# Half-size products from the fifth block on in the two feed-forward layers, with another way to make the first output weights

## The chip, the cores and the metric

The program runs on one core of a Trainium2 chip. The metric is device time in microseconds (us) from launch to end; the figure for the kernel before is the median of three runs. The engines are named as the profile names them: PE multiplies matrices, PEld loads weights into it, DVE and ACT work element by element, POOL is the general engine that here issues the adding DMA, and SP issues the plain loads and stores. A line such as L485 is a line of the profiled kernel's file.

## What is computed

The reference is one layer of a decoder over 512 prompt tokens and 8 x 4 new tokens: a half-step SwiGLU feed-forward (FF1), a token mixer (RWKV-7 heads beside differential attention), a second half-step SwiGLU (FF2), each between two root-mean-square norms. The change lies in the two feed-forwards:

```python
def rms_norm(x, g, eps):
    xf = x.astype(jnp.float32)
    y = xf * lax.rsqrt(jnp.mean(xf * xf, axis=-1, keepdims=True) + eps)
    return (y * g.astype(jnp.float32)).astype(x.dtype)

def swiglu(x, w_in, w_out):
    gate, up = jnp.split(x @ w_in, 2, axis=-1)
    return (jax.nn.silu(gate) * up) @ w_out
```

`x` has 544 rows of 1024, `w_in` is 1024 x 5632, `w_out` 2816 x 1024, all float32.

## The kernel before, in words

**Tiles and exactness.** The tokens lie along the free dimension in two halves of 272, so each product is a matmul of a 128 x 128 piece of weight with 128 x 272 of input. A float32 product is made of three products in the round format fp32r: `whi` is the weight rounded (ACT copy), `wlo` the rest (raw minus `whi`), and the input is split in the same way into high and low (`split`, L164 to L166: ACT copy, DVE subtract). `dot` issues for each of the pieces high x high (L148) and high x low (L149) and, after all of these, low x high (L154). So a weight's low is asked for late in its product.

**A feed-forward** (`ff`, from L431) has 22 blocks of 128 hidden columns; a block needs a gate column block and an up column block. Blocks are gathered in `GROUPS`; after the blocks of a group, the group's hidden tiles `hd0`, `hd1` (one set for each token half, each split into high and low) are multiplied with the group's rows of `w_out` (`products`, L377) and added to the eight output tiles `y` of each half. In the first group the output is copied from PSUM by ACT (L615), in later ones it is added by DVE (L620).

**The two kinds of block.** The first group's blocks are multiplied plainly: 2 weights x 2 halves x 8 pieces x 3 = 96 matmuls a block. Blocks 0 and 1 go through `opening`, blocks 2 to 5 through the loop at L569 (two blocks a pass, `ws` holds their four weights, token half outside, block inside). All other blocks go through `seven` (L509), a form of Strassen's and Winograd's method: the block's gate and up columns against the upper and lower half of the 1024 rows make a 2 x 2 matrix of weights, and the input's halves by tokens and rows another; seven products of half the depth (`product`, 4 pieces x 3 = 12 matmuls each, 84 in all) and some additions give the same four results.

**What `seven` needs.** Of the weights, `load` brings `b` (called `wraw`), `t1` (two 256 KB loads of the same piece on SP's queue, then one adding DMA of 512 KB on POOL's queue, L473) and `b22`; `factors` makes the high and low of `b`, `b22`, `t1` and of `t2`, a sum that DVE makes (L497, L498). The low of `b` is made by an ACT copy with scale -1 onto which a DMA on POOL's queue adds the weight from memory (L494, L495); the other lows are DVE subtractions (L487). Of the input it needs seven sets: `scaled` (L412) multiplies the rows of `h` by norm and gain in place (L417) and splits three of four quarters into the tiles `fa`; `mixtures` (L425) makes four sums and differences (L430) and splits them into `sh`, `sl`. Both are generators that are stepped by other work: `scaled` by four steps behind each hidden tile of the passes of blocks 4 and 5 (L588 to L590), `mixtures` by two steps behind each output copy of the first group (L616).

**What sets the order.** The lines give a program order; a scheduler that simulates a timeline then sets each engine's order, from priorities, from due dependences and from `after(ins)`, which lets what follows be issued only after `ins`. Tiles of one name share a few buffers: four `whi`/`wlo`, three `wraw`, three `t1`, six hidden tiles in each half. A new weight's high and low wait until the one four places back has been read last.

**Names the change touches**: `GROUPS`, `split`, `weights` (whose argument `added` chooses the ACT copy and adding DMA at L121 and L122 over the DVE subtraction at L124), `products`, `mixtures`, `hidden`, `load`, `factors`, `seven`, the loop at L569 and `finish` (L613). `begin` and `midway` are what the two feed-forwards do beside their opening blocks: FF1 stores the input and prepares a table at `midway`.

Of the kernel before, what the change touches and what calls it, by code (L numbers as in the profile page):

```python
# [22 lines left out]
GROUPS = ((0, 6), (6, 11), (11, 16), (16, 22))  # L23
# [29 lines left out]
def build(ctx, tc, A):  # L53
# [109 lines left out]
    def split(pool, src, name, n=HALF, into=None, **kw):  # L163
        hi, lo = into or [pool.tile([128, n], FR, name=name + p, **kw) for p in "hl"]  # L164
        S.activation(hi, src, AF.Copy)
        V.tensor_tensor(lo, src, hi.bitcast(FT), op=OP.subtract)  # L166
# [14 lines left out]
    turn, last, latest, root = [0], [None], [None], [None]  # L181
# [195 lines left out]
    def products(wsrc, x, y, finish, per=1, wx=None, apart=False):  # L377
# [21 lines left out]
    def combined(pre, h, pool, xp):  # L399
# [25 lines left out]
        def mixtures():  # L425
            for k in range(KH):
                a11, a12, a21, a22 = h[0][:, k], h[0][:, KH + k], h[1][:, k], h[1][:, KH + k]
                for i, (dst, p, q, op) in enumerate(((a22, a22, a21, OP.subtract), (a21, a11, a21, OP.add),
                                                     (a11, a22, a11, OP.subtract), (a12, a12, a11, OP.add))):
# [8 lines left out]
    def ff(win, wout, pre, h, done, xp, end, lead=(), begin=None, midway=None, ahead_of_end=None):  # L438
        with ExitStack() as st:
# [7 lines left out]
            hid, made = [[], []], [None]  # L447
            wt = None

            def hidden(s, g, u, sign=1.0):  # L450
                S.activation(g, g, AF.Silu, scale=sign)
                made[0] = V.tensor_tensor(u, u, g, op=OP.mult).ins
# [10 lines left out]
            def load(j):  # L463
# [4 lines left out]
                for i in range(2):  # L468
                    nc.sync.dma_start(t1[:, i], win[j, 1, :, :512])
# [3 lines left out]
                G.dma_start(t1, bass.AP(tensor=src.tensor, offset=src.offset,  # L473
                                        ap=[[1024, 128], [128 * 1024 + 512, 2], [1, 512]]), accum_op=OP.add)
                loaded[j] = raw, t1, b22

            def factors(j):
# [16 lines left out]
                S.activation(lo, raw, AF.Copy, scale=-1.0)  # L494
                G.dma_start(lo, win[j, 0], accum_op=OP.add)  # L495
# [14 lines left out]
            def seven(j):  # L510
# [23 lines left out]
                r = half(abank)  # L534
                product(r, t1, 1, s3)
                g1 = add(gu_tile("ga"), r, u2)
                q = half(bank)
                product(q, t1, 0, s1)
# [13 lines left out]
            for gi, (j0, j1) in enumerate(GROUPS):  # L552
                if gi == 0:
# [17 lines left out]
                    behind = [None, None]  # L571
                    for j in range(2, j1, 2):
                        if midway and j == 4:
                            midway()
                        ws = [[weights(win[i, n], 1024, added=begin is None and i == 3) for n in range(2)] for i in (j, j + 1)]
# [1077 lines left out]
```

## Time and profile before

| | us |
|---|---|
| median of three runs | 1195.15 |
| the runs | 1193.9, 1195.15, 1203.37 |
| the profiled execution | 1195.1 |
| its span (first to last instruction) | 1193.3 |

The mean clock that PE was granted in the profiled execution was 0.989 of full speed. The span is what the profile resolves; 1.8 us lie outside it. In the page, the first line of an engine gives its busy time, the share of the span and its instructions; the groups give for each line what an engine did, how long one took, and how long the engine stood idle just before them and what ended the wait. In the view of windows each row has the start and end, the length, then busy time with number of instructions of PE, PEld, DVE, ACT and POOL, the clock that PE was granted, the share of the DMA engines in use and GB/s. In the timeline each row has start, length, engine, line, operation, tiles, count, and in brackets the idle time ahead and what ended it.

Two stretches matter: FF1's first group and its output (blocks from the start to 84.95 us, output from 84.95 to 122.50 us), and the same in FF2 (output from 875.27 to 912.82 us).

### The profile page before, as it was taken

The page shows a single profiled execution, that of the slowest core. Times are in us where ns is not written, and L with a number is a line of the kernel's source. Part 1 is how long each engine was busy: PE and PEld are TensorE (multiplying, and loading weights), DVE is VectorE, ACT ScalarE, POOL GpSimd, SP SyncE. Part 2 cuts the span into 40 slices and gives each one's busy share as a digit, 9 for nine tenths or more (in the row PEclk, how much of TensorE's full clock was granted, in tenths as well). Part 3 has the DMA queues.
Part 4 walks back from the last instruction along what each step waited for, and adds up shares of the span by engine and source line. Part 5 has one row for each costly group of instructions (what it writes and reads, how often), then busy time and mean ns, then how long its engine had stood idle before and what let it go on. Part 6 is the DMA issues. An engine that isn't in the chain of part 4 may idle for free. (4 is left out here: it accounts for less than half of the span.)

```text
span 1193.3 us, 25431 instructions
## 1 busy us (share of the span) xinstructions
PE 1166.6 (98%) x10020; PEld 1103.5 (92%) x10020; DVE 821.2 (69%) x1878; ACT 583.6 (49%) x1081; POOL 169.5 (14%) x228
## 2 busy tenths in 40 slices
PE   8999999999999999999999999999999999999995
PEld 8999999999999999989897645999999999999995
DVE  8794684775875777778525658788784766857856
ACT  6455552643645664443214546567455634525530
POOL 0001110110101165531000021100001201101001
PEclk9999999999999998899999999999999999999998
DMA  7328895884847456789426486554259876857532
GB/s 262 108 67 240 218 212 122 198 205 114 189 162 211 117 155 175 223 228 257 118 56 209 143 321 214 192 190 132 72 152 230 210 181 154 216 144 181 116 116 75
DMA packets 86089, 205.42 MB, mean 172 GB/s; under 512 B 9144, under 2 KB 20152, under 8 KB 84562
## 3 DMA queue, kind: packets, MB, share of 16 engines
q1 hardware_dynamic: 65954, 149.69, 37.7%
q0 software_dynamic: 17712, 49.65, 23.4%
q10 hardware_dynamic: 2304, 4.46, 1.0%
q8 instruction: 79, 1.29, 0.4%
q14 instruction: 40, 0.33, 0.1%
HBM read 186.12 MB, written 18.95 MB: 172 GB/s over the span
## 5 line engine op out<-in xcount | busy, mean ns | idle before, releaser
L118 ACT ACTIVATE whi<-wraw 128x1024 fp32r<-128x1024 f32 (+2 forms) x127 | 116.8, 923 | 164.3 <-PE mm L149 75.3
L148 PE MATMUL mm<-xh,whi 128*128 128x272 f32 x456 | 121.3, 296 | 3.1 <-ACT whi L645 2.0
L149 PE MATMUL mm<-xl,whi 128*128 128x272 f32 x456 | 120.6, 294 | 0.0
L124 DVE TENSOR_TENSOR wlo<-wraw,whi 128x1024 fp32r<-128x1024 f32 (+2 forms) x100 | 100.6, 1008 | 17.7 <-ACT whi L118 16.7
L148 PEld LDWEIGHTS mm<-xh,whi 128*128 128x128 f32 x456 | 87.7, 193 | 4.5 <-ACT whi L645 2.2
L473 POOL DMA_DIRECT2D t<-in_ff_in_dram x32 | 38.8, 1213 | 362.7 <-DMA t<-in_ff_in_dram 139.4
L149 PEld LDWEIGHTS mm<-xl,whi 128*128 128x128 f32 x456 | 87.8, 193 | 0.4 <-DVE xl L282 0.2
L519 DVE TENSOR_TENSOR ga<-pb,ga 128x272 f32<-128x272 f32 x140 | 61.1, 436 | 23.6 <-PE pb L508 21.2
L154 PE MATMUL mm<-xh,wlo 128*128 128x272 f32 x456 | 69.3, 291 | 0.2 <-DMA wlo<-in_w_in_dram 0.2
L620 DVE TENSOR_TENSOR y<-mm,y 128x272 f32<-128x272 f32 x66 | 29.0, 440 | 54.9 <-PE mm L154 54.5
L505 PE MATMUL pb<-sh,t1h 128*128 128x272 f32 x256 | 66.7, 288 | 0.0
L506 PE MATMUL pb<-sl,t1h 128*128 128x272 f32 x256 | 66.6, 287 | 0.0
L149 PE MATMUL mm<-hd1l,whi 128*128 128x272 f32 x242 | 62.7, 289 | 1.0 <-DVE hd1l L166 1.0
L154 PEld LDWEIGHTS mm<-xh,wlo 128*128 128x128 f32 x456 | 61.9, 190 | 0.9 <-DMA wlo<-in_w_in_dram 0.5
L485 ACT ACTIVATE t1h<-t 128x1024 fp32r<-128x1024 f32 x32 | 34.0, 1061 | 58.7 <-issue 32.5
L149 PE MATMUL mm<-hd0l,whi 128*128 128x272 f32 x242 | 62.6, 288 | 0.0
L148 PE MATMUL mm<-hd0h,whi 128*128 128x272 f32 x242 | 62.2, 288 | 0.0
L148 PE MATMUL mm<-hd1h,whi 128*128 128x272 f32 x242 | 62.1, 289 | 0.0
L148 PE MATMUL pb<-xh,whi 128*128 128x272 f32 x232 | 61.3, 294 | 0.0
L149 PE MATMUL pb<-xl,whi 128*128 128x272 f32 x232 | 60.5, 291 | 0.0
L505 PE MATMUL pb<-fa,whi 128*128 128x272 f32 x216 | 56.2, 288 | 0.0
L506 PE MATMUL pb<-fa,whi 128*128 128x272 f32 x216 | 56.2, 288 | 0.0
(510 smaller groups left out, 3625.1 us busy)
## 6 DMA issues: line engine op xcount, KB each, us to landing
wraw<-in_ff_in_dram SPq DMA_DIRECT2D x55, 512.0 KB, 4.7
wlo<-in_ff_in_dram POOLq DMA_DIRECT2D x34, 512.0 KB, 7.3
t<-in_ff_in_dram SPq DMA_DIRECT2D x64, 256.0 KB, 3.6
t<-in_ff_in_dram POOLq DMA_DIRECT2D x32, 512.0 KB, 6.0
wraw<-in_w_in_dram SPq DMA_DIRECT2D x26, 512.0 KB, 8.0
wlo<-in_w_in_dram POOLq DMA_DIRECT2D x25, 512.0 KB, 8.3
wraw<-in_ff_out_dram SPq DMA_DIRECT2D x32, 384.0 KB, 3.1
wraw<-in_ff_out_dram SPq DMA_DIRECT2D x32, 320.0 KB, 3.2
```

The source lines that it names most:

```text
L118: S.activation(hi, raw, AF.Copy)
L124: V.tensor_tensor(lo, raw, hi.bitcast(FT), op=OP.subtract)
L148: T.matmul(ps, hi, xs[k][0], start=k == 0, stop=False)
L149: latest[0] = T.matmul(ps, hi, xs[k][1], start=False, stop=False).ins
L154: latest[0] = T.matmul(ps, wcols(w, k0 + k)[1], xs[k][0], start=False, stop=k == n - 1).ins
L473: G.dma_start(t1, bass.AP(tensor=src.tensor, offset=src.offset, ap=[[1024, 128], [128 * 1024 + 512, 2], [1, 512]]), accum_op=OP.add)
L485: S.activation(hi, src, AF.Copy)
L505: T.matmul(ps, c, x[k][0], start=k == 0, stop=False)
L506: T.matmul(ps, c, x[k][1], start=False, stop=False)
L519: V.tensor_tensor(dst, p, q, op=op)
L620: V.tensor_tensor(y[s][m], ps, y[s][m], op=OP.add)
```

## The change

**Groups.** The first group has four blocks rather than six, the others six. Blocks 4 and 5 go from 96 to 84 matmuls, and the loop at L569 is gone but for its first pass; the output weights of the first group are 128 x 512 rather than 128 x 768 (256 KB rather than 384 KB).

**Input.** `scaled` is stepped behind the hidden tiles of blocks 2 and 3, each step after the low of the hidden tile before (`made[0]`, now set in `split`). `mixtures` goes set by set rather than piece by piece; its steps come after the last low made.

**First output weights.** Their lows are made with `added`: an ACT copy with scale -1 and an adding DMA of 256 KB on POOL's queue, eight in each feed-forward, in place of a DVE subtraction.

**First seven-product block.** Its `t1` is summed by two DVE additions of 128 x 512 rather than by the adding DMA (and one of two loads falls away), and the low of its `b` is a DVE subtraction.

**Order in `seven`.** The products `r` and `q` (of `t1`) come ahead of the first of `t2`.

```diff
-GROUPS = ((0, 6), (6, 11), (11, 16), (16, 22))
+GROUPS = ((0, 4), (4, 10), (10, 16), (16, 22))
...
-        V.tensor_tensor(lo, src, hi.bitcast(FT), op=OP.subtract)
+        made[0] = V.tensor_tensor(lo, src, hi.bitcast(FT), op=OP.subtract).ins
...
-            ws.append(weights(wsrc(u), per * n * 128, wx and wx[u // 2]))
+            ws.append(weights(wsrc(u), per * n * 128, wx and wx[u // 2], added))
...
-            for k in range(KH):
-                a11, a12, a21, a22 = h[0][:, k], h[0][:, KH + k], h[1][:, k], h[1][:, KH + k]
-                for i, (dst, p, q, op) in enumerate(((a22, a22, a21, OP.subtract), (a21, a11, a21, OP.add),
+            for i in range(4):
+                for k in range(KH):
+                    a11, a12, a21, a22 = h[0][:, k], h[0][:, KH + k], h[1][:, k], h[1][:, KH + k]
...
-                for i in range(2):
+                first = j == GROUPS[0][1]
+                for i in range(1 if first else 2):
                     nc.sync.dma_start(t1[:, i], win[j, 1, :, :512])
...
+                if first:
+                    V.tensor_tensor(t1[:, 1], t1[:, 0], b22, op=OP.add)
+                    V.tensor_tensor(t1[:, 0], t1[:, 0], raw[:, :512], op=OP.add)
+                else:
+                    G.dma_start(t1, bass.AP(tensor=src.tensor, offset=src.offset,
+                                            ap=[[1024, 128], [128 * 1024 + 512, 2], [1, 512]]), accum_op=OP.add)
...
-                S.activation(lo, raw, AF.Copy, scale=-1.0)
-                G.dma_start(lo, win[j, 0], accum_op=OP.add)
+                if j == GROUPS[0][1]:
+                    V.tensor_tensor(lo, raw, hi.bitcast(FT), op=OP.subtract)
+                else:
+                    S.activation(lo, raw, AF.Copy, scale=-1.0)
+                    G.dma_start(lo, win[j, 0], accum_op=OP.add)
...
+                r = half(abank)
+                product(r, t1, 1, s3)
+                q = half(bank)
+                product(q, t1, 0, s1)
                 p = half(acc_tile)
                 product(p, t2, 0, s2)
...
-                    for j in range(2, j1, 2):
-                        if midway and j == 4:
-                            midway()
+                    if midway:
+                        midway()
...
+                            with after(behind[0] if behind else None):
+                                for _ in range(4):
+                                    next(scaled, None)
+                            behind.append(made[0])
+                            del behind[:-1]
...
-                        for _ in range(2):
-                            next(mixtures, None)
+                        with after(made[0] if m else None):
+                            for _ in range(2):
+                                next(mixtures, None)
...
-                products(lambda m: wout[:, m, off:off + n * 128], group, y, finish, wx=late if lastg else None, apart=lastg)
+                products(lambda m: wout[:, m, off:off + n * 128], group, y, finish, wx=late if lastg else None, apart=lastg, added=not gi)
```

Over the whole program PE issues 48 matmuls fewer (12 in each of two blocks of two feed-forwards), DVE 14 element-by-element operations more, ACT 30 more, POOL 20 DMAs more and SP 6 more.

**The first place: the last hidden tile of FF1's first group.** DVE makes its low, `hd1l`. Before, the rows of DVE that lead to it are these (L430 and L408 are `mixtures`, L452 the product of gate and up, L166 the low):

```order
L408 TENSOR_TENSOR sl2_1_1280<-h0_85,sh2_1_1279 128x272
L408 TENSOR_TENSOR sl3_0_1219<-h0_85,sh3_0_1218 128x272
L430 TENSOR_TENSOR h0_85<-h0_85 128x272
L452 TENSOR_TENSOR up_1135<-up_1135,ga_1134 128x272
L408 TENSOR_TENSOR sl2_2_1346<-h0_85,sh2_2_1345 128x272
L430 TENSOR_TENSOR h0_85<-h0_85 128x272
L408 TENSOR_TENSOR sl2_3_1412<-h0_85,sh2_3_1411 128x272
L408 TENSOR_TENSOR sl3_1_1285<-h0_85,sh3_1_1284 128x272
L408 TENSOR_TENSOR sl3_2_1351<-h0_85,sh3_2_1350 128x272
L166 TENSOR_TENSOR hd1l_1141<-up_1135,hd1h_1140 128x272
```

After, the same place has these (L593 takes up from PSUM, L453 multiplies, L417 and L410 are `scaled`, L431 and L408 `mixtures`):

```order
L593 TENSOR_TENSOR up_871<-mm_821,rpre1_311 128x272
L431 TENSOR_TENSOR h1_158<-h1_158 128x272
L410 SCALAR_TENSOR_TENSOR fa_185<-h1_158,fa_184 128x272
L431 TENSOR_TENSOR h1_158<-h1_158 128x272
L410 SCALAR_TENSOR_TENSOR fa_185<-h1_158,fa_185 128x272
L453 TENSOR_TENSOR up_871<-up_871,ga_870 128x272
L431 TENSOR_TENSOR h1_158<-h1_158 128x272
L408 TENSOR_TENSOR sl0_0_915<-h1_158,sh0_0_914 128x272
L431 TENSOR_TENSOR h1_158<-h1_158 128x272
L408 TENSOR_TENSOR sl0_1_920<-h1_158,sh0_1_919 128x272
L166 TENSOR_TENSOR hd1l_877<-up_871,hd1h_876 128x272
```

There the scaling of the input is now among what stands ahead of the low, and `mixtures` has only begun, where before it was nearly through.

PE's rows around that low's first reader (L149, `hd1l_1141`), before; `mm_1192`, `mm_1258` and `pb_1324` are the first three outputs of the second token half, `wlo_1160` the first output weight's low:

```order
L149 MATMUL pb_1324<-hd1l_834,whi_1290 128x272
L148 MATMUL pb_1324<-hd1h_1076,whi_1290 128x272
L149 MATMUL pb_1324<-hd1l_1077,whi_1290 128x272
L148 MATMUL mm_1192<-hd1h_1140,whi_1158 128x272
L148 MATMUL mm_1258<-hd1h_1140,whi_1224 128x272
L148 MATMUL pb_1324<-hd1h_1140,whi_1290 128x272
L149 MATMUL mm_1192<-hd1l_1141,whi_1158 128x272
L154 MATMUL mm_1192<-hd1h_635,wlo_1160 128x272
L154 MATMUL mm_1192<-hd1h_643,wlo_1160 128x272
L154 MATMUL mm_1192<-hd1h_773,wlo_1160 128x272
L154 MATMUL mm_1192<-hd1h_833,wlo_1160 128x272
L154 MATMUL mm_1192<-hd1h_1076,wlo_1160 128x272
```

After, with `hd1l_877`, `wlo_896` and `pb_923`, `mm_978`, `mm_1033` in their places:

```order
L149 MATMUL mm_1033<-hd1l_659,whi_1004 128x272
L148 MATMUL mm_1033<-hd1h_812,whi_1004 128x272
L149 MATMUL mm_1033<-hd1l_813,whi_1004 128x272
L148 MATMUL mm_1033<-hd1h_876,whi_1004 128x272
L149 MATMUL pb_923<-hd1l_877,whi_894 128x272
L154 MATMUL pb_923<-hd1h_650,wlo_896 128x272
L154 MATMUL pb_923<-hd1h_658,wlo_896 128x272
L154 MATMUL pb_923<-hd1h_812,wlo_896 128x272
L154 MATMUL pb_923<-hd1h_876,wlo_896 128x272
L149 MATMUL mm_978<-hd1l_877,whi_949 128x272
L154 MATMUL mm_978<-hd1h_650,wlo_951 128x272
L154 MATMUL mm_978<-hd1h_658,wlo_951 128x272
```

PE holds back the second half's outputs until the low has come, as before; it now comes as the 46th matmul of this output rather than the 70th, and the first output weight's low is read last by the 50th.

**The second place: the fifth output weight of FF1's first group,** the first that needs the buffer of another. ACT's rows there before; L615 are output copies, `whi_1422` is the fifth weight's high, and L485 belongs to the first block of seven products:

```order
L165 ACTIVATE hd1h_1140<-up_1135 128x272
L406 ACTIVATE sh3_3_1416<-h0_85 128x272
L118 ACTIVATE whi_1422<-wraw_1420 128x768
L615 ACTIVATE y1_0_194<-mm_1192 128x272
L118 ACTIVATE whi_1468<-wraw_1466 128x768
L615 ACTIVATE y1_1_195<-mm_1258 128x272
L615 ACTIVATE y1_2_196<-pb_1324 128x272
L485 ACTIVATE b22h_1634<-b22_1614 128x512
L118 ACTIVATE whi_1514<-wraw_1512 128x768
L615 ACTIVATE y0_2_188<-mm_1294 128x272
L615 ACTIVATE y0_3_189<-mm_1360 128x272
```

After, `whi_1114` and `wlo_1116` are the fifth weight's (L623 the output copies, L406 the highs of `mixtures`):

```order
L406 ACTIVATE sh1_0_969<-h1_158 128x272
L406 ACTIVATE sh1_1_974<-h1_158 128x272
L118 ACTIVATE whi_1114<-wraw_1112 128x512
L406 ACTIVATE sh1_2_993<-h1_158 128x272
L623 ACTIVATE y1_0_194<-pb_923 128x272
L121 ACTIVATE wlo_1116<-wraw_1112 128x512
L118 ACTIVATE whi_1149<-wraw_1147 128x512
L406 ACTIVATE sh1_3_998<-h1_158 128x272
L623 ACTIVATE y1_1_195<-mm_978 128x272
L121 ACTIVATE wlo_1151<-wraw_1147 128x512
```

The low is now ACT's as well, and stands behind an output copy and a high of `mixtures`. POOL's queue, whose first rows before are these (L689 ends the table, L473 adds onto `t1`, L495 onto `wlo`):

```order
L689 DMA rb_d_162<-rb_1_849 128x2560
L473 DMA t1_1611<-in_ff1_in_dram 128x2x512
L473 DMA t1_1619<-in_ff1_in_dram 128x2x512
L473 DMA t1_1761<-in_ff1_in_dram 128x2x512
L495 DMA wlo_1631<-in_ff1_in_dram 128x1024
L473 DMA t1_1903<-in_ff1_in_dram 128x2x512
L495 DMA wlo_1773<-in_ff1_in_dram 128x1024
L495 DMA wlo_1915<-in_ff1_in_dram 128x1024
L473 DMA t1_2045<-in_ff1_in_dram 128x2x512
```

has after the change the eight lows of the first output ahead of all adds of the blocks (L698 ends the table, L122 are the new adds):

```order
L698 DMA rb_d_162<-rb_1_569 128x2560
L122 DMA wlo_896<-in_ff1_out_dram 128x512
L122 DMA wlo_951<-in_ff1_out_dram 128x512
L122 DMA wlo_1006<-in_ff1_out_dram 128x512
L122 DMA wlo_1061<-in_ff1_out_dram 128x512
L122 DMA wlo_1116<-in_ff1_out_dram 128x512
L122 DMA wlo_1151<-in_ff1_out_dram 128x512
L122 DMA wlo_1186<-in_ff1_out_dram 128x512
L122 DMA wlo_1221<-in_ff1_out_dram 128x512
L479 DMA t1_1267<-in_ff1_in_dram 128x2x512
L479 DMA t1_1408<-in_ff1_in_dram 128x2x512
L504 DMA wlo_1420<-in_ff1_in_dram 128x1024
```

The first adding DMA of the seven-product blocks now belongs to the second such block (`t1_1267`). PE reads `wlo_1116` from its 93rd matmul of the output on.

More of the change, by code (lines that the diff above doesn't have):

```diff
@@ L179, in xbank @@
         return px.tile([128, 512], FT, name="pb")
[L181 removed]
+    turn, last, latest, root, made = [0], [None], [None], [None], [None]
     def acc_tile():
@@ L375, in opening, with products @@
         ends.clear()
-    def products(wsrc, x, y, finish, per=1, wx=None, apart=False):
+    def products(wsrc, x, y, finish, per=1, wx=None, apart=False, added=False):
         n = len(x[0])
```

44 lines of the change are left out of this document (17 added, 27 removed).

## The prediction, as it was put on record

> **What bounds the kernel now.** I read the page first, then the view of windows over the first feed-forward, then PE's timeline there.
>
> ```profile
> span 1193.3 us, 25431 instructions
> PE 1166.6 (98%) x10020; PEld 1103.5 (92%) x10020; DVE 821.2 (69%) x1878; ACT 583.6 (49%) x1081; POOL 169.5 (14%) x228
> 40.00:60.00 20.00, 20.00 (x162) 20.00 (x162) 13.82 (x30) 8.70 (x18) 0.00 (x0) 1.00 0.24 74
> 80.00:100.00 20.00, 19.24 (x151) 18.80 (x151) 17.71 (x42) 12.06 (x28) 1.28 (x1) 1.00 0.48 132
> 140.00:160.00 20.00, 20.00 (x162) 20.00 (x161) 16.35 (x32) 12.99 (x20) 3.65 (x5) 1.00 0.96 227
> ```
>
> PE is busy 98% of the span, and in the feed-forwards' steady stretches both PE and its weight loads fill all 20.00 us. There a matmul left out is time gained, and other engines count only where they make PE wait. The window from 80 to 100 us is the exception: PE lacks 0.76 us, its loader 1.20, with DVE busy 17.71. PE's own rate and the places where it lacks come from its timeline:
>
> ```profile
> 71.95 1.16 PE L154 MATMUL mm<-xh,wlo 128*128 128x272 f32 x8
> 74.95 1.16 PE L154 MATMUL pb<-xh,wlo 128*128 128x272 f32 x8
> 84.95 0.29 PE L148 MATMUL mm<-hd0h,whi 128*128 128x272 f32 x1
> 94.80 0.39 PE L149 MATMUL mm<-hd1l,whi 128*128 128x272 f32 x1 [0.52 <-DVE hd1l L166]
> 122.50 0.29 PE L505 MATMUL mm<-fa,whi 128*128 128x272 f32 x1
> 875.27 0.29 PE L148 MATMUL mm<-hd0h,whi 128*128 128x272 f32 x1
> 885.12 0.39 PE L149 MATMUL mm<-hd1l,whi 128*128 128x272 f32 x1 [0.52 <-DVE hd1l L166]
> 912.82 0.29 PE L505 MATMUL mm<-fa,whi 128*128 128x272 f32 x1
> ```
>
> The first two rows are the same place in two successive products of 24 matmuls: 3.00 us, so 0.125 us a matmul (the 0.29 of a row is its length in the pipeline). The first group's output has 8 weights x 2 halves x 6 blocks x 3 = 288 matmuls, 36.0 us at that rate. It takes 122.50 - 84.95 = 37.55 us in FF1 and 912.82 - 875.27 = 37.55 in FF2. So 1.55 us are lost in each, and the bracketed rows say on what: the low of the last hidden tile.
>
> **Step 1: two blocks by seven products.** 96 - 84 = 12 matmuls less for each of blocks 4 and 5, in two feed-forwards: 48 x 0.125 = **-6.0 us**, on the path. The additions that seven products need on DVE lie beside PE, if DVE keeps up (step 5).
>
> **Step 2: the old wait.** Why is the low late?
>
> ```profile
> 90.00:95.00 5.00, 4.24 (x31) 3.80 (x31) 5.00 (x15) 2.22 (x6) 0.76 (x1) 1.00 0.54 184
> 880.00:885.00 5.00, 4.36 (x33) 3.92 (x31) 5.00 (x16) 2.22 (x6) 0.38 (x1) 1.00 0.55 184
> 92.20 0.43 DVE L452 TENSOR_TENSOR up<-up,ga 128x272 f32<-128x272 f32 x1
> 94.31 0.43 DVE L166 TENSOR_TENSOR hd1l<-up,hd1h 128x272 fp32r<-128x272 f32 x1
> 66.08 1.49 DVE L408 TENSOR_TENSOR fa<-h,fa 128x272 fp32r<-128x272 f32 x4
> 57.00 1.73 DVE L417 SCALAR_TENSOR_TENSOR h<-h,gains,rpre 128x272 f32<-128x272 f32 x4
> ```
>
> DVE is busy all 5.00 us there: five rows of `mixtures` stand between the tile's product (92.20) and its low (94.31). In the changed order PE asks for this low 45 matmuls, 5.6 us, into the output. The shorter first group starts it 2 x 96 x 0.125 = 24.0 us sooner, at 60.95 in FF1; the low is wanted at 66.57. I laid DVE's rows of the changed order out in line from 40.2 us, when the first of block 2's products is whole: 59 instructions, at 0.354 us for a 128x272 operation (the x4 row: (1.49 - 0.43) / 3), 0.43 for one with gains (1.73 / 4), take about 21.6 us, and DVE idles some 3 us of the way on PE's products. The low is then done at 65.2 to 65.6, about 1 us before it is wanted, and in FF2, where fewer stand ahead, about 1.9 us before. So the wait goes: 2 x 1.55 = **-3.1 us**. What hides DVE's work is that margin; each 0.36 us of delay past it would cost as much, and at worst the 3.1 are paid again.
>
> **Step 3: the new wait.** The lows of the eight output weights no longer come from DVE but from an ACT copy and an adding DMA. The first four have free buffers and many us; the fifth is the tight one. Its buffer is free when PE has read the first weight's low for the last time, 50 matmuls = 6.25 us into FF1's output. From there ACT has to make the high, a high of `mixtures`, an output copy, then the copy with scale -1:
>
> ```profile
> 98.46 0.63 ACT L485 ACTIVATE b22h<-b 128x512 fp32r<-128x512 f32 x1 [0.33 <-DMA b<-in_ff_in_dram]
> 58.44 1.38 ACT L406 ACTIVATE fa<-h 128x272 fp32r<-128x272 f32 x4
> 87.41 0.40 ACT L615 ACTIVATE y<-mm 128x272 f32<-128x272 f32 x1 [0.75 <-PE mm L154]
> 109.56 1.05 ACT L494 ACTIVATE wlo<-wraw 128x1024 fp32r<-128x1024 f32 x1
> 110.91 0.88 POOL L495 DMA_DIRECT2D wlo<-in_ff_in_dram  x1 [0.71 <-ACT wlo L494]
> ```
>
> A 128x512 copy takes 0.63 us alone and about 0.53 in a row of such; the high of `mixtures` 0.32 ((1.38 - 0.42) / 3), the output copy 0.30 in the same way; with 0.2 for the release that is 0.53 + 0.32 + 0.30 + 0.53 + 0.2 = 1.9. The last two rows show POOL's queue issuing 0.3 us after the copy ends (110.91 - 110.61). So the DMA is issued at 6.25 + 1.9 + 0.3 = 8.45 us. PE asks for the low at its 93rd matmul, 92 x 0.125 = 11.50 us. If the DMA takes L from issue to landing, PE waits L - 3.05. In FF2 PE's order frees the buffer at 55 matmuls and asks at 104: issue at 6.88 + 2.2 = 9.05, asked at 13.0, wait L - 3.95. Later weights have margins of 6 us and more, and get the fifth's wait on top: they wait for nothing more unless L passes about 8.5.
>
> No adding DMA of 256 KB into these tiles ran before, so L is bounded by neighbours, here the groups of DMA issues (size, then median us to landing) and the landing lines of two tile views, of `t` in FF2's start and of `wlo`:
>
> ```profile
> t<-in_ff_in_dram SPq DMA_DIRECT2D x64, 256.0 KB, 3.6
> twl<-in_w_in_dram POOLq DMA_DIRECT2D x1, 256.0 KB, 5.8
> sgl<-in_w_in_dram POOLq DMA_DIRECT2D x1, 256.0 KB, 7.1
> wlo<-in_ff_in_dram POOLq DMA_DIRECT2D x34, 512.0 KB, 7.3
> DMA to landing us min/median/max: 3.0/5.9/8.9
> DMA to landing us min/median/max: 5.2/7.6/10.2
> ```
>
> Below, a plain load of the same size on SP's queue: 3.6 in the middle, 3.0 at best. Above, the double size on the same queue: 7.3 in the middle, 10.2 at worst. Nearest are the two adds of just this size on POOL's queue, 5.8 and 7.1; I take 5.8, since nothing else is to be fetched with haste while the output runs. PE then waits 2.75 us in FF1 and 1.85 in FF2: **+4.6 us**. With 7.1 it is 4.05 + 3.15 = +7.2; with 3.0 nothing; with 10.2 it is 7.15 + 6.25 = +13.4.
>
> [...]
>
> **Step 4: the first seven-product block.** It drops an adding DMA (512 KB) and a load, and DVE makes two sums and a low instead:
>
> ```profile
> L497 DVE TENSOR_TENSOR wraw<-t,b 128x512 f32<-128x512 f32 x32 | 22.1, 692 | 41.1 <-ACT wlo L494 19.1 <-DMA b<-in_ff_in_dram 15.8 <-DMA t<-in_ff_in_dram 4.5
> L487 DVE TENSOR_TENSOR wlo<-wraw,whi 128x1024 fp32r<-128x1024 f32 x32 | 39.0, 1218 | 8.0 <-ACT whi L485 7.6
> ```
>
> That is 2 x 0.69 + 1.22 = 2.6 us of DVE, while DVE is freed of eight lows. It stands about 2 us before the block's products ask for it, by the same way of laying out, more if step 3's wait comes. I take nothing; with that cover gone it would cost up to 2.6 us in each feed-forward. Moving `r` and `q` ahead of `p` changes what PE reads, not how much, and gives `t2`, which DVE makes last, 24 matmuls = 3.0 us more: nothing while there is no wait on it, and it guards against one. SP's queue gets six more, smaller loads; PE waits on no plain load of these stages before, so nothing.
>
> **Step 5: scaling sooner.** `scaled` (16 x 0.43 us, 12 splits) runs from block 2 on. It fills DVE from 45 to 65 us, where the window above shows 13.82 of 20 used. Its price is in step 2's margin.
>
> **Step 6: the mixer.** It does the same work, in an order that the scheduler has reshuffled. What can change is the clock: by the windows it is granted half speed twice.
>
> ```profile
> 460.00:464.00 4.00, 4.00 (x17) 3.50 (x16) 3.61 (x16) 3.65 (x6) 1.27 (x1) 0.50 0.80 323
> 464.00:468.00 4.00, 4.00 (x25) 4.00 (x24) 0.84 (x2) 0.00 (x0) 0.00 (x0) 0.69 0.00 2
> 484.00:488.00 4.00, 4.00 (x17) 3.50 (x17) 3.52 (x13) 3.38 (x5) 2.61 (x5) 0.50 1.03 298
> 488.00:492.00 4.00, 4.00 (x25) 4.00 (x25) 1.55 (x7) 0.00 (x0) 0.00 (x0) 0.71 0.73 163
> ```
>
> In 460 to 468 PE loses 4 x 0.50 + 4 x 0.31 = 3.2 us, in 484 to 492 3.2 again. Both come after a cluster of small matmuls. The changed order has such clusters too, so I take nothing; one dip fewer or more is 3.2 us either way.
>
> [...]
>
> **The sum**, against the profiled execution's 1195.1 us (span 1193.3 and 1.8 around it; the median of the three is 1195.15, so the two agree): -6.0 - 3.1 + 4.6 = -4.5, **1190.6 us**.
>
> **The rivals.**
> - No new wait: L under 3.05 us. For it: plain loads of this size land in 3.0 to 3.6. Against: no add onto `wlo` landed under 5.2. Time 1195.1 - 9.1 = 1186.0. [...]
> - Slower than before: the adds land late. The waits are L - 3.05 and L - 3.95; they eat the 9.1 us gained from L = 8.05 on. For it: the double size reached 10.2 us, and the eight adds share POOL's queue. Against: the median of the double size is 7.3, and the DMA engines are half used in that window (0.48). At 10.2: 1186.0 + 13.4 = 1199.4.
> - The mixer's dips: one fewer or more on top of the forecast, 1187.4 or 1193.8. For it: the order there is new. Against: the clusters remain.
> - DVE's margin gone: `hd1l` late as before, +3.1, 1193.7.
>
> **How the numbers follow.** The forecast case (L from 5 to 7.1, dips as before) has 0.50, and lies within 1189 to 1193.2; no new wait 0.17; dips 0.15 (both signs alike); DVE's margin 0.06; slower by late adds 0.12. The range reaches from no wait with one dip less, 1186.0 - 3.2 = 1182.8, to the late adds' 1197 (L = 9.0: 1186.0 + 11.0); L beyond that or a loss I have not seen is left out, as is more than one gain on top of no wait. One per cent, 11.95 us, is about what a measurement of this kernel can tell from no change: under 1183.2 is faster, over 1207.1 slower. Faster needs no wait and a dip less or more: 0.10. Slower needs L of 14 us, or several losses: 0.04. Within: 0.86.
>
> **What would show it.** In the changed kernel's profile: 48 matmuls fewer; the first output with 192 matmuls, 24.0 us plus its wait, 26.8 in FF1 and 25.9 in FF2, and PE's wait in it ended by the DMA onto `wlo` at the fifth output weight; no wait on `hd1l`; adds of 256 KB landing in about 5.8 us; the two dips. I am wrong if PE waits there on ACT or `hd1l`, if the adds land under 4 us or over 8, or if the mixer's length moves by more than 3 us.

## The result and the profile after

The changed kernel takes 1207.26 us (median of 7; 1206.17 to 1210.85) where the kernel before takes 1195.15 (median of 7). The ratio is 1.0099 with a 95% interval of [1.0075, 1.0122]: about one per cent slower. The forecast was 1190.6 with a range to 1197.0, so it was wrong in size and in sign. The profiled execution is one of 1206.17 us, span 1204.4; the one before had 1193.3.

The page of the changed kernel, first the span, the engines and the queue of instructions (packets, MB), then the group of matmuls that read the high part of `t1` in the blocks of seven products:

```profile
span 1204.4 us, 25404 instructions
PE 1166.6 (97%) x9972; PEld 1103.0 (92%) x9972; DVE 824.6 (68%) x1892; ACT 593.9 (49%) x1111; POOL 186.2 (15%) x248
q8 instruction: 78, 1.28, 0.4%
L514 PE MATMUL pb<-sh,t1h 128*128 128x272 f32 x288 | 76.6, 292 | 6.0 <-DVE ga L528 5.9
```

PE has 48 matmuls less and still the same busy time, so some ran at a lower clock (its mean is 0.985, before 0.989); and L514 waits 5.9 us on L528, an addition of DVE on which the profile before shows no wait of PE. The view of waits gives PE's and DVE's waits that matter (engine, line, what ended the wait: us, times, longest):

```profile
PE pb L514 <- DVE ga L528: 5.9, 5, 2.1
PE mm L154 <- DMA wlo<-in_ff_out_dram: 3.3, 2, 1.8
PE pb L987 <- issue: 1.7, 1, 1.7
DVE wraw L506 <- DMA b<-in_ff_in_dram: 28.1, 15, 4.4
```

The second row is the new wait that was forecast, the first and the third were not. Before, DVE's line of the same sum (L497) waited for `b`, the load of `b22`, for

```profile
DVE wraw L497 <- DMA b<-in_ff_in_dram: 15.8, 13, 2.1
```

PE's timeline gives the stages, at the places shown of before, and the waits in them:

```profile
61.63 0.29 PE L148 MATMUL mm<-hd0h,whi 128*128 128x272 f32 x1
74.86 0.40 PE L154 MATMUL mm<-hd0h,wlo 128*128 128x272 f32 x1 [1.46 <-DMA wlo<-in_ff_out_dram]
87.92 0.30 PE L514 MATMUL pb<-sh,t1h 128*128 128x272 f32 x1
147.98 0.36 PE L514 MATMUL pb<-sh,t1h 128*128 128x272 f32 x1 [1.30 <-DVE ga L528]
857.15 0.29 PE L148 MATMUL pb<-hd0h,whi 128*128 128x272 f32 x1
874.01 0.39 PE L154 MATMUL mm<-hd0h,wlo 128*128 128x272 f32 x1 [1.85 <-DMA wlo<-in_ff_out_dram]
922.25 0.36 PE L514 MATMUL pb<-sh,t1h 128*128 128x272 f32 x1 [2.09 <-DVE ga L528]
```

FF1's first output takes 87.92 - 61.63 = 26.29 us (24.0 at PE's 0.125 us a matmul). The six blocks behind it take 70.67 us, to 158.59, where their 528 matmuls are worth 66.0; before, the 444 matmuls at that place took 55.52 for 55.5. That is the loss that the forecast lacked. In FF2 the same two stages lie partly in one another; together they take 98.28 us for 720 matmuls, 90.0, with PE's clock below full in both:

```profile
857.15:887.21 30.06, 28.21 (x211) 0.94 0.83 211
887.21:955.43 68.22, 66.13 (x514) 0.97 0.93 228
```

(columns of this view when asked for PE alone: length, PE busy with instructions, granted clock, DMA share, GB/s). The clock alone costs an estimated 30.06 x 0.06 + 68.22 x 0.03 = 3.9 us there; it fell after the two waits at 874 and 922 (0.74 from 876 to 880 us, 0.53 from 924 to 926).

Against the profile of before, FF1 ends 3.8 us later, the mixer is 1.1 longer (411.5 against 410.4), FF2 to the end 6.2: 11.1 in all, the difference of the spans. In FF1 the sum is -3.0 (24 matmuls) - 1.55 (the old wait) + 0.7 (later start of the output) + 2.3 + 4.7 + 0.7 (rest); in FF2 -3.0 - 1.55 + 1.0 + 8.3 + 1.5.

### The profile page after: what moved, and what is told of

Same layout as the page of the kernel before. It is cut to its first block, busy times and chain, and to the rows that moved or that the text cites. A ratio compares the mean times of both kernels' runs of the same rounds, so it can differ in the third digit from the quotient of the medians.

```text
span 1204.4 us, 25404 instructions
## 1 busy us (share of the span) xinstructions
PE 1166.6 (97%) x9972; PEld 1103.0 (92%) x9972; DVE 824.6 (68%) x1892; ACT 593.9 (49%) x1111; POOL 186.2 (15%) x248
## 4 chain that ended last, share of the span: by engine, by line
PE 71%; DMA 11%; DVE 8%; issue 5%; ACT 2%; SPq 2%; POOL 1%; DVEq 0%; POOLq 0%; ACTq 0%
PE mm L148 8%; PE mm L154 8%; PE mm L149 8%; PE pb L514 5%; PE pb L515 5%; PE pb L517 5%; PE pb L154 4%; DMA b<-in_ff_in_dram 4%; PE pb L148 4%; PE pb L149 4%; PE mm L515 2%; PE mm L514 2%; PE mm L517 2%; DMA t<-in_ff_in_dram 1%; DVE ga L528 1%
## 5 line engine op out<-in xcount | busy, mean ns | idle before, releaser
L148 PE MATMUL mm<-xh,whi 128*128 128x272 f32 x376 | 100.8, 298 | 3.5 <-ACT whi L654 2.1
L149 PE MATMUL mm<-xl,whi 128*128 128x272 f32 x376 | 99.4, 294 | 0.0
L124 DVE TENSOR_TENSOR wlo<-wraw,whi 128x768 fp32r<-128x768 f32 (+1 forms) x76 | 79.9, 1053 | 11.3 <-ACT whi L118 8.4
L491 ACT ACTIVATE whi<-wraw 128x1024 fp32r<-128x1024 f32 x36 | 38.2, 1061 | 90.4 <-DVE wraw L507 40.4
L514 PE MATMUL pb<-sh,t1h 128*128 128x272 f32 x288 | 76.6, 292 | 6.0 <-DVE ga L528 5.9
L148 PEld LDWEIGHTS mm<-xh,whi 128*128 128x128 f32 x376 | 72.4, 193 | 4.9 <-ACT whi L654 2.3
L149 PEld LDWEIGHTS mm<-xl,whi 128*128 128x128 f32 x376 | 72.3, 193 | 0.7 <-DVE xl L282 0.2
L528 DVE TENSOR_TENSOR ga<-pb,ga 128x272 f32<-128x272 f32 x156 | 66.0, 436 | 2.0
L506 DVE TENSOR_TENSOR wraw<-t,b 128x512 f32<-128x512 f32 x36 | 24.9, 692 | 58.2 <-DMA b<-in_ff_in_dram 28.1
L504 POOL DMA_DIRECT2D wlo<-in_ff_in_dram x34 | 36.3, 1067 | 173.0 <-ACT wlo L503 172.4
L514 PE MATMUL pb<-fa,whi 128*128 128x272 f32 x236 | 61.4, 288 | 0.0
L514 PEld LDWEIGHTS pb<-sh,t1h 128*128 128x128 f32 x288 | 54.9, 191 | 7.1 <-issue 4.8
L149 PE MATMUL mm<-hd1l,whi 128*128 128x272 f32 x232 | 60.5, 289 | 0.0
L149 PE MATMUL mm<-hd0l,whi 128*128 128x272 f32 x230 | 59.6, 288 | 0.0
L154 PE MATMUL mm<-xh,wlo 128*128 128x272 f32 x376 | 57.2, 293 | 0.0
```

Source lines behind the costliest of these rows:

```text
L124: V.tensor_tensor(lo, raw, hi.bitcast(FT), op=OP.subtract)
L148: T.matmul(ps, hi, xs[k][0], start=k == 0, stop=False)
L149: latest[0] = T.matmul(ps, hi, xs[k][1], start=False, stop=False).ins
L154: latest[0] = T.matmul(ps, wcols(w, k0 + k)[1], xs[k][0], start=False, stop=k == n - 1).ins
L514: T.matmul(ps, c, x[k][0], start=k == 0, stop=False)
L528: V.tensor_tensor(dst, p, q, op=op)
```

## The experiments

The table has, for each kernel, the two stages in FF1 and FF2 together (from the first matmul of the first output to the first of the second; 90.0 us at PE's rate, for the kernel before and the two built on it 91.5), the mixer's length (from FF1's last matmul to FF2's first), the median, and the ratio to the kernel before, which ran beside it: its own medians went from 1193.9 to 1197.6 us, so ratios are compared rather than medians. The stages and the mixer are of one profiled execution. Two kernels with the same order (the changed one and `after_shift`) differ by 1.7 and 2.5 us in the stages, so less than that says nothing.

| kernel | FF1 | FF2 | mixer | median | ratio, interval |
|---|---|---|---|---|---|
| before | 93.07 | 93.07 | 410.4 | 1195.15 | |
| changed | 96.96 | 98.28 | 411.5 | 1207.26 | 1.0099 [1.0075, 1.0122] |
| order | 93.38 | 94.27 | 415.6 | 1203.28 | 1.0032 [1.0001, 1.0063] |
| b22_3 | 92.59 | 95.19 | 414.5 | 1200.70 | 1.0029 [0.9999, 1.0060] |
| noadd | 96.36 | 95.97 | 413.4 | 1205.34 | 1.0050 [1.0023, 1.0078] |
| order_noadd | 94.42 | 94.19 | 420.0 | 1204.23 | 1.0026 [0.9999, 1.0053] |
| after_shift | 95.23 | 95.77 | 408.8 | 1200.97 | 1.0033 [1.0005, 1.0060] |
| before_shift | 93.07 | 93.07 | 413.0 | 1202.23 | 1.0061 [1.0026, 1.0095] |
| all3 | 93.07 | 93.98 | 413.0 | 1200.92 | 1.0024 [0.9991, 1.0056] |
| all3_shift | 94.37 | 95.10 | 413.4 | 1194.89 | 0.9972 [0.9943, 1.0001] |
| before_rq | 93.18 | 93.18 | 419.5 | 1196.92 | 0.9991 [0.9962, 1.0021] |
| b22_shift | 94.13 | 94.78 | 406.9 | 1196.85 | 1.0014 [0.9994, 1.0034] |
| b22_order_shift | 93.75 | 94.34 | 412.6 | 1197.66 | 0.9995 [0.9969, 1.0020] |
| two_shift | 97.25 | 99.46 | 405.8 | 1200.36 | 1.0035 [1.0012, 1.0057] |
| early_shift | 95.03 | 94.16 | 411.1 | 1197.95 | 1.0030 [1.0004, 1.0055] |
| early_b22_shift | 94.57 | 95.14 | 409.9 | 1197.26 | 1.0012 [0.9993, 1.0032] |
| early_all_shift | 92.09 | 92.38 | 406.6 | 1187.67 | 0.9941 [0.9916, 0.9965] |

**What stands behind PE's wait on a DVE addition.** The changed kernel's SP and DVE around the wait at 147.98, in order of time:

```profile
138.02 0.68 DVE L493 TENSOR_TENSOR b22l<-b,b22h 128x512 fp32r<-128x512 f32 x1
138.72 0.33 SPq L473 DMA_DIRECT2D b<-in_ff_in_dram  x1
144.22 0.69 DVE L506 TENSOR_TENSOR wraw<-t,b 128x512 f32<-128x512 f32 x1 [3.77 <-DMA b<-in_ff_in_dram]
144.83 1.22 DVE L493 TENSOR_TENSOR t1l<-t,t1h 128x1024 fp32r<-128x1024 f32 x1
147.39 0.92 DVE L528 TENSOR_TENSOR ga<-pb,ga 128x272 f32<-128x272 f32 x2
```

`b22` has two buffers. The load of the next but one starts when DVE has made a low out of the present one (138.02, issued at 138.72) and lands 5.5 us later. DVE does a few short additions meanwhile and then stands still for 3.77 us, since the next instruction in its order (L506, the sum for `t2`) needs that load. Behind L506 in DVE's order are the additions of the block that PE is working on, which free a PSUM bank that PE wants next. So here a late load stops DVE (3.77 us), and DVE stops PE (1.30 us). Two parts of that chain can be undone: what PE asks for behind DVE (the order of products), and the load. A third theory was that the new adding DMAs crowd the engines.

*order*: the product of t2 first again, as before.

```diff
+                p = half(acc_tile)
+                product(p, t2, 0, s2)
+                add(u2, p, u2)
                 r = half(abank)
                 product(r, t1, 1, s3)
+                g1 = add(gu_tile("ga"), r, u2)
                 q = half(bank)
                 product(q, t1, 0, s1)
-                p = half(acc_tile)
-                product(p, t2, 0, s2)
-                add(u2, p, u2)
-                g1 = add(gu_tile("ga"), r, u2)
```

> The changed kernel with one part undone: in the seven products, the product of t2 comes ahead of r and q again. In the changed kernel the six blocks behind FF1's first output take 70.67 us (66.0 at PE's rate) and PE waits there for a DVE addition, 3.3 us in brackets. Theory A (the order of products: r's bank is held over three products and asked for 12 matmuls sooner, so it is not free when DVE stands still for a load): the waits on the additions go, these blocks take 66 to 67 us in both feed-forwards, first output still 26.3, total about 1197. Theory B (the loads of b22 through two buffers are the loop that sets the pace) and theory C (the eight adds of 256 KB crowd the DMA engines): blocks still 70 us, total 1204 to 1207.

The stages fell by 3.6 and 4.0 us, and no wait of PE on L528 is left, though DVE stands still for `b` longer than in the changed kernel:

```profile
DVE wraw L506 <- DMA b<-in_ff_in_dram: 35.1, 20, 4.8
```

*b22_3*: a third buffer.

```diff
-                b22 = wt.tile([128, 512], FT, name="b22", bufs=2)
+                b22 = wt.tile([128, 512], FT, name="b22", bufs=3)
```

> The changed kernel with three buffers for b22 in place of two. Theory B (DVE waits for a b22 whose load could not start before the one two blocks back was split): DVE's waits on the load of b in FF1's blocks, 3 to 4.4 us each, go, and with them PE's; these blocks take 66 to 67 us, total about 1197. Theory A: the bank is still asked for too soon behind DVE's rows of the next block; at least half of the 4.7 us in these blocks stays, total above 1201. Theory C: the load is late because the DMA engines are crowded, and starts sooner into the same crowd: little change, 1204 or more.

DVE's wait goes from 28.1 us to

```profile
DVE wraw L506 <- DMA b<-in_ff_in_dram: 3.7, 3, 2.7
```

and FF1's blocks from 70.67 to 66.79 us, with no wait on L528. The two cures cut the same chain at two places, and the intervals of both ratios lie below that of the changed kernel. How much each is worth is less sure: against `after_shift`, which has the changed kernel's order, FF1 is 1.9 us shorter in `order` and 2.6 in `b22_3`. The median of 1200.7 stays above what was expected, as with `order`: the rest is in the mixer (below).

*noadd* and *order_noadd*: the first output's lows by DVE again; the second with the order of products as well.

```diff
-                products(lambda m: wout[:, m, off:off + n * 128], group, y, finish, wx=late if lastg else None, apart=lastg, added=not gi)
+                products(lambda m: wout[:, m, off:off + n * 128], group, y, finish, wx=late if lastg else None, apart=lastg)
```

> The changed kernel with the lows of the first output weights made by DVE again, no adding DMA. PE's wait on the DMA onto wlo at the fifth output weight (1.46 us in FF1, 1.85 in FF2, and the half clock behind the latter) goes under every theory: first output 24 to 25 us. Theory C: the waits in the blocks behind go too, total about 1194 or less. Theories A and B: the blocks still take 70 us, or more since DVE has eight more rows; total 1200 to 1204.

> Both undone: the product of t2 first, and no adding DMA for the first output weights. Theory A: no wait of over 1 us is left in either feed-forward, and the sum of the prediction without the new wait holds: about 1186 to 1190. Theories B and C as sole cause: at least 1194.

FF1's first output falls to 24.21 us, so its wait is what the adding DMAs cost. The blocks don't gain; they take 72.15 and 70.21 us, and in both PE now waits for the adding DMA onto the second block's low of `b`, here in `noadd`:

```profile
102.41 0.39 PE L517 MATMUL pb<-fa,wlo 128*128 128x272 f32 x1 [2.18 <-DMA wlo<-in_ff_in_dram]
```

DVE stands still for `b` for 34.0 us in `noadd`, and PE still waits on L528 there, at most 0.8 us at a time. So crowding by the adds falls as the cause of DVE's standing; how long PE then waits may depend on it.

**The order alone, on the kernel before.** *before_rq* makes the edit of `order` the other way round.

> The kernel before with one part of the change alone: in the seven products, r and q ahead of the product of t2. By this DVE's order has the sum of the next block's t2, which waits for a load of b22, ahead of the additions that free r's bank, as in the changed kernel. Theory A (the order of products makes PE wait wherever DVE stands still for b22): waits of PE on DVE's additions, 0.5 to 1.5 us a block, appear in the blocks behind the first output, 57 to 60 us in place of 55.5; total 3 to 10 us over before. Theory B (it takes the late loads of the changed start as well; the longer first output of before gives them time): blocks 55.5 to 56, total as before within 2 us.

Its blocks take 55.64 us in place of 55.52. So the order alone does no harm. But DVE did not stand still for long in this run, 6.3 us for `b` in all and never over 1.8 (15.8 and 2.1 before), so it does not show the order beside a late load; `order` does.

**The mixer.** Three facts pointed to PE's instruction stream: the changed kernel and the four above have a wait on "issue" of 1.6 to 2.2 us in the burst of 32x32 matmuls at 580 us and a lowered clock behind it; the profile before has neither; and the page has 78 packets of 16 KB on q8, the queue of instructions, beside 9972 matmuls and as many weight loads, 255.7 of them to a packet (79 packets before, 253.7 to each). The places before and after (a burst has 56 matmuls; the row behind a break shows only its first few):

```profile
579.06 1.07 PE L978 MATMUL pb<-ld,tmp 32*32 32x32 f32 x56
...
579.55 0.82 PE L987 MATMUL pb<-ld,tmp 32*32 32x32 f32 x40
582.06 0.31 PE L987 MATMUL pb<-ld,tmp 32*32 32x32 f32 x8 [1.70 <-issue]
```

*after_shift* and *before_shift* put matmuls that nobody reads at FF1's table, 12 in the changed kernel and 52 in the kernel before:

```diff
+        pad = abank()
+        for _ in range(12):
+            T.matmul(pad[:32, :32], ones[:32, :32], ones[:32, :32], start=True, stop=True)
         for c0, c1 in ((0, 512), (512, NRB)):
```

> The changed kernel with 12 idle float32 matmuls of 32x32 (48 PE instructions with their weight loads) at the table in FF1, which nothing reads. The order of every engine's other rows is the same. Theory D: 24 matmuls fewer in FF1 move PE's instruction stream by 48 against the blocks of 256 in which its instructions are fetched (16 KB each in the trace), and in the mixer's burst of 32x32 matmuls at 580 us PE now runs dry for 1.7 us and then falls to half clock for 10.2 us, which the profile of before does not show. With the stream moved back: no wait on issue at that burst, no dip of 10 us behind it, mixer 405 to 410 us in place of 411.5, total 3 to 7 us less, about 1201. Theory E (the mixer's other order makes that wait, or it is chance): the wait stays, total 1206 to 1208.

> The kernel before with 52 such idle matmuls (104 with their two passes, 208 instructions with the loads; 208 is 256 less 48, so the stream behind them lies in the blocks as in the changed kernel). About 1.8 us of PE time for them in FF1. Theory D: the wait on issue of about 1.7 us and a dip behind it appear in the mixer's burst of 32x32 matmuls, total 5 to 9 us over before. Theory E: no such wait, total 1.8 us over before.

The page counts each idle matmul twice (x9972 became x9996), so 12 of them stand for the 24 matmuls that FF1 lost. The break in the burst moved as counted. In the changed kernel it came after the 40th of 56, shifted after the 16th and cost almost nothing; shifted by 104, the kernel before has it after the 40th, with the wait, as if breaks lay 128 matmuls apart (16 - 104 + 128), 256 with their weight loads (first two rows `after_shift`, then `before_shift`):

```profile
577.75 0.44 PE L990 MATMUL pb<-ld,tmp 32*32 32x32 f32 x16
578.39 0.28 PE L990 MATMUL pb<-ld,tmp 32*32 32x32 f32 x6 [0.20 <-issue]
...
578.56 0.82 PE L981 MATMUL pb<-ld,tmp 32*32 32x32 f32 x40
580.68 0.28 PE L981 MATMUL pb<-ld,tmp 32*32 32x32 f32 x6 [1.31 <-issue]
```

and the windows of 580 to 600 us read, in the order before, changed, after_shift, before_shift:

```profile
580.00:600.00 20.00, 20.00 (x260) 1.00 0.20 64
580.00:600.00 20.00, 18.30 (x210) 0.74 0.22 71
580.00:600.00 20.00, 20.00 (x253) 1.00 0.15 45
580.00:600.00 20.00, 19.32 (x206) 0.74 0.16 51
```

Where the wait is, 20 us at 0.74 of full clock cost an estimated 20 x 0.26 = 5.2 us. The median fell by 6.3 us in the one and rose by 4.7 in the other, of which an estimated 2.1 are the idle matmuls themselves (104 in the page's count, at the burst's 0.82 us for 40); the first two kernels' ratios have intervals apart, and that of `before_shift` lies above 1 by 3 to 11 us, idle matmuls included. The lowered clock is not bound to a long wait alone: `before_rq`, whose stream was not moved, had a wait of 0.74 us and 0.66 in this window of its profile, and `all3_shift` 0.83 behind 0.21 us. So the place of the break sets the wait (0 to 0.74 us behind the 13th to 17th matmul or where no break shows, 1.3 to 2.2 behind the 37th to 40th). The clock fell in this window in all seven profiles with the long wait and in these two of the ten others.

The profiles are one execution each, and the mixer's length differs by 9 us between two with the same stream (`before` and `before_rq`). But every execution on record has its span and mean clock, and span x (1 - clock) estimates what the clock took. Its mean over a kernel's executions is 16.8 to 19.7 us in the seven kernels with the late break, 10.9 to 17.1 in the ten others: about 4 us apart. The rest, span x clock, is what work and waits took: 1186.5 us in the changed kernel, 1183.8 in `order`, 1180.7 in `b22_3`, 1180.3 to 1181.0 before.

**Combinations.** *all3* is order, b22_3 and noadd together, *all3_shift* has the 12 idle matmuls too; *b22_shift* and *b22_order_shift* keep the adding DMAs; *two_shift* is all3_shift with the low of `b` by DVE in two blocks:

```diff
-                if j == GROUPS[0][1]:
+                if j - GROUPS[0][1] in (0, 1):
                     V.tensor_tensor(lo, raw, hi.bitcast(FT), op=OP.subtract)
```

> Product of t2 first, three buffers for b22, and no adding DMA for the first output weights. Theory B with A as the lesser part: no wait of over 0.5 us in FF1's and FF2's blocks; first output 24.2, blocks 66 to 66.5 us in both feed-forwards, FF1's last output at about 384.5 us (391.4 in the changed kernel, 387.7 before). Total by D about 1196, since the wait on issue in the mixer stays. If something else bounds the blocks (DVE's own work), they stay above 67.5.

> The same with the 12 idle matmuls that move PE's instructions back by 48. If B and D both hold, this is the sum of the prediction without its new wait: feed-forwards 6 to 7 us shorter than before, mixer as before: about 1188 to 1191, faster than before. If D falls, as all3.

> The changed kernel with three buffers for b22 and the 12 idle matmuls; all else as in the change, the first output's adding DMAs too. The run with three buffers took 1200.7, with 10.2 us of half clock behind the wait on issue. By B and D: blocks 66 to 67 us, first output 25.8 as there, and no such wait on issue: 1193 to 1196.

> As the one before, with the product of t2 first as well. If order and buffers cure the same wait, no gain over it: 1193 to 1196, blocks 66 to 67. If the order adds something of its own (theory A beside B), blocks 66.0 to 66.3 and 1 to 3 us less.

> Product of t2 first, three buffers for b22, no adding DMA for the first output weights, the 12 idle matmuls, and the low of b made by DVE in the second seven-product block too. Without the latter PE waits 1.6 to 2.5 us in each feed-forward on the adding DMA onto that low. If the late adding DMA is all that is left there: blocks 66 to 67.5 us, total 1188 to 1192, the fastest. If PE then waits on the next one (loads of that stage late as a whole, since the first output is 13 us shorter than before and its start is when they begin): blocks 68 or more, total as without it, 1194 to 1196.

The shift was again worth 6.0 us (all3), and 3.9 with b22_3, but in both the intervals of the two ratios overlap. None of them reached the sum without waits: `order_noadd` was expected at 1186 to 1190 us, `all3_shift` at 1188 to 1191 and `two_shift` at 1196 at most; they took 1204.23, 1194.89 and 1200.36. With the adds, `b22_shift` has the blocks at 66.21 us and the first output at 27.92; without them the first output is 24.2 and the wait stands on the second block's low; where that low was made by DVE, on the third's, and longer:

```profile
113.23 0.59 PE L517 MATMUL pb<-fa,wlo 128*128 128x272 f32 x1 [4.64 <-DMA wlo<-in_ff_in_dram]
```

**Why something is always late.** The first loads of `t1` in FF1, before and after:

```profile
89.52 0.90 SPq L469 DMA_DIRECT2D t<-in_ff_in_dram  x2
...
74.05 0.45 SPq L471 DMA_DIRECT2D t<-in_ff_in_dram  x1
```

`t1` and `b22` lie where the input `h` lay, and wait until `mixtures` is done with it. Before, the first blocks' loads began 122.50 - 89.52 = 33.0 us ahead of the first block; now 87.92 - 74.05 = 13.9. The *early* kernels give `t1` its three buffers beside `h`:

```diff
+            wq = pool("wq", st2)
             gu = pool("gu", st2)
...
-                t1 = wt.tile([128, 2, 512], FT, name="t1", bufs=3)
+                t1 = wq.tile([128, 2, 512], FT, name="t1", bufs=3)
```

> The changed kernel with the 12 idle matmuls, and with t1's three buffers in memory of their own rather than where the input h lay, so that t1's loads and their adding DMA need not wait for the end of the mixtures. Beside it stands after_shift: blocks 69.03 us in FF1, waits on DVE's additions of up to 0.85 us, first output 26.2, median 1200.97. Theory F (the blocks' loads begin only at 71 to 76 us, 14 us ahead of the first block against 33 before, and all that they wait for is that late start): with 3 MB of them moved ahead, blocks 66 to 67 us and total 1194 to 1198. Theory B alone (the loop through b22's two buffers): blocks 68.5 to 69.5 as in after_shift.

> The same with three buffers for b22. Beside it stands b22_shift: blocks 66.21 us, but first output 27.92 with two waits of 1.5 and 1.7 us on the adding DMAs of the output weights, median 1196.85. Theory F with the adds late because they share the DMA engines with t1's loads: first output 24.5 to 26, blocks 66 to 66.3, total 1192 to 1195. If the adds are late by their own chain alone (buffer, ACT, queue): first output as there, 26 to 28.

> Product of t2 first, three buffers for b22, no adding DMA for the first output weights, the idle matmuls, and t1's buffers of their own. Beside it stands all3_shift: first output 24.21, blocks 70.16 with a wait of 2.35 us on the adding DMA onto the second block's low of b, median 1194.89. Theory F: that wait goes or falls under 1 us, blocks 66 to 67.5, total 1188 to 1192, clearly faster than before. If that low is late because of wraw's three buffers, which the output weights hold until DVE has made their lows, and not of t1: blocks 69 to 71 and total as there.

Alone, or with the third `b22`, the early `t1` brought nothing that the stages show (95.03 and 94.57 in FF1 against 95.23 and 94.13): the wait went to the second block's low. With all three edits it did: 92.09 and 92.38 (94.37 and 95.10 in `all3_shift`), 1187.67 us, ratio 0.9941 [0.9916, 0.9965]. The two stages differ by about what one profile can tell; the mean of span x clock fell too, from 1180.0 us to 1175.1. That is the one version clearly faster than both kernels. Its largest wait in the stages is still

```profile
99.09 0.40 PE L518 MATMUL pb<-fa,wlo 128*128 128x272 f32 x1 [1.60 <-DMA wlo<-in_ff_in_dram]
```

so the short lead is part of the cause, but not all of it: `wraw`, whose three buffers the output weights hold until 71 us in the changed kernel and until 73 in this one, was not moved, and what its loads would give was not tried.

## Why the prediction was wrong, step by step

- **Step 1, 48 matmuls:** right; x10020 became x9972.
- **Step 2, the old wait:** right; no wait of PE on `hd1l` is left, and without the adds the first output takes 24.21 us, 0.21 over its matmuls.
- **Step 3, the new wait:** right in place and cause in FF1. Its parts there: issue 69.73 - 61.63 = 8.1 us into the output (8.45 forecast, of which 0.2 for the release was an estimate that no row shows), landing 5.1 us later (5.8), a stage of 26.29 us (26.8). In FF2 PE waited 1.85 us as forecast, but that is luck: the fifth weight's add, issued at 865.99, landed in 4.3 us, just in time, and PE waited on the sixth's, issued at 867.64, which took 6.3. The step had given later weights margins of 6 us and more. And the clock behind the wait was not counted.
- **Step 4, the first seven-product block and the loads:** this failed. It was "I take nothing", with a cover of about 2 us for the one block that the diff names, and "nothing" for the order of `r` and `q`, which "guards against" a wait. The cover was named for one operation, not for the chain of loads behind it. Its lead went from 33 to 14 us; DVE's standing for `b`, which the row of L497 in that step already gives as 15.8 us before, went to 28.1; and the order that was to give `t2` more time made PE ask for a bank behind that. That the shorter lead alone made DVE stand longer is not shown: with `t1` early it still stood 21.6 us (`early_shift`). The profiles put the step at 3.6 to 4.4 us in FF1 (`order`, `b22_3`) and 3.1 to 4.0 in FF2; against `after_shift` it is 1.9 to 2.6 and 0.6 to 1.5. By span x clock over all executions it is 2.7 us (`order`) to 5.8 (`b22_3`) in both together, where the step had 0.
- **Step 5, scaling sooner:** right; the margin held.
- **Step 6, the mixer:** failed in kind. It weighed a dip more or less at 3.2 us, both signs alike, with "I take nothing". What moved was PE's place in its instruction stream, the same in each kernel with 24 matmuls less in FF1, and with the clock behind it the runs put it at 2.5 to 6.3 us. The profiled pair hides this by luck: its mixers differ by only 1.1 us, because the one before lost 6.4 us in its two dips, the changed one 1.7 there and 5.2 at 580 us.
- **The rivals:** "slower by late adds" had the sign, by another mechanism; the adds landed in 4.5 to 7.3 us between 60 and 80 us (6.1 in the median), under the 8.05 from which this rival would have cost more than the gain.

Of the gain of 9.1 us the runs show a part. The best version has 0.9941 of the time before, some 7 us less; by span x clock 5.2 us of that are work and waits (1175.1 against 1180.3), the rest is clock. The change lost more than that at three places, of which one was forecast: the first outputs' waits, the blocks behind them, and the clock behind the waits and in the mixer.

## What to carry to other kernels

When a stage is shortened, ask what was loading behind it: the loads of the next stage can lose the lead that it gave them (here from 33 to 14 us), and the first to feel it may be an engine that stands still for a load with another stage's releases queued behind. Order products so that what PE asks for next does not hang on that engine. And a change in the number of instructions can move a stall into a far, unchanged part of a program (here 1.70 us at 580 us, with 24 matmuls less in FF1); a few idle instructions that leave every order as it is tell that apart from a new order of work.

## What was not expected of the hardware

In a burst of 32x32 matmuls (40 in 0.82 us) PE stood still on "issue" for 1.70 us in the changed kernel, or for 0.20 in `after_shift`, depending on how many matmuls came ahead of the burst, with the order of work the same. Waits of PE of about 2 us were followed by a clock near half in the changed kernel's FF2 (0.50 from 875 to 878 us behind 1.85 us, 0.53 from 924 to 926 behind 2.09), and not by any after 1.46 us in FF1 (1.00 from 76 to 84 us); but the length does not decide it, for a wait of 0.74 us in `before_rq` had 0.66 in the window of 580 to 600 us behind it, and one of 1.60 at 99.09 us in `early_all_shift` had 1.00 from 100 to 120.
